# A rotary embedding on one core: storing the first batch in five parts of growing row width

## The chip, the cores and the metric

The kernel runs on one core of a Trainium2 chip. The metric is the device time of one execution in microseconds (us). "Span" is the part of it between the first and the last instruction in the trace; the device time is some 2 us longer. Ratios are computed as the mean time of one kernel's runs over that of the other's of the same rounds, so they are not quite the ratio of the medians quoted. The record gives spans to 0.1 us. The profile gives times in us from the start of the span.

## The reference

```python
x: [8, 2048, 8, 64] f32      cos, sin: [2048, 32] f32
x1, x2 = x[..., :32], x[..., 32:]
out1 = x1 * cos - x2 * sin
out2 = x1 * sin + x2 * cos
out  = concatenate([out1, out2], -1)
```

Each of the eight batches is 4 MB. The kernel must read 34.1 MB (with the tables) and write 33.6 MB.

## The kernel before

A batch lies in SBUF as 128 partitions of 8192 floats, so one row of a whole-batch DMA is 32 KB. There are five buffers, and the rotation is computed in place.

```python
HD = 512; ROW = 8192; UNIT = 2048; NBUF = 5      # floats per partition

def load(b):                                      # loads: SP queue
    for lo, n in spans([UNIT, UNIT, 2 * UNIT] if b == 0 else [ROW]):
        nc.sync.dma_start(out=xt[:, lo:lo+n], in_=xv[b, :, lo:lo+n])
        ...                                       # cos, sin after the first part

def store(b, lo, n):                              # stores: ScalarE's queue
    nc.scalar.dma_start(out=ov[b, :, lo:lo+n], in_=xts[b][:, lo:lo+n])

for b in range(NBUF): load(b)
...                                               # tables; rotate(): see below
for b in range(B):
    done = 0
    outs = list(spans([2 * UNIT, UNIT, UNIT] if b == last else [ROW]))
    for lo, n in spans(pieces(b)):                # batch 0: 2 HD, 2 HD, 3 x UNIT
        rotate(b, lo, n)
        done = lo + n
        while outs and sum(outs[0]) <= done:
            store(b, *outs.pop(0))
    if b + NBUF <= last: load(b + NBUF)           # reuses a stored buffer
```

`rotate` makes two GpSimd products with the sine (line 121), one VectorE product with the cosine (line 128) and mostly one VectorE addition back into the batch (line 135). A few pieces are added by TensorE and copied back by ScalarE.

## Time and profile before

| | before |
|---|---|
| device time, median of 6 runs | 164.25 us (164.15 to 164.58) |
| profiled span | 162.0 us |
| bytes moved | 67.65 MB |
| last VectorE instruction ends | 155.3 us |
| last store lands | 161.05 us |

The lines that carry the reading are shown in the prediction below. The page's slices cut the span in 40; a digit is the busy share in tenths. The windows table gives busy time of each engine, then the clock, the DMA share and GB/s. It books a packet at the packet's start. A packet of 32 KB takes 1.2 us, so windows of a few us scatter by some 30 GB/s around the rate. Where this document speaks of "us lost", the rate comes instead from the trace's record of each DMA packet, with its bytes spread over its duration: every stretch of 2 us between 14 and 150 us that is under 425 GB/s counts as (433 - rate)/433 x 2 us.

### The profile page before, as it was taken

To read this page: it belongs to the slowest core of one execution; us is meant where nothing else is said; L and a number is where in the kernel's file an instruction comes from. 1 tells how busy PE (TensorE), PEld (TensorE's weight loads), DVE (VectorE), ACT (ScalarE), POOL (GpSimd) and SP (SyncE) were. 2 spreads that over 40 slices of the span, in tenths; PEclk is the share of its full clock that TensorE was granted. 3 is DMA by queue.
4 is the path that set the end of the run, shared out by engine and by line. 5 is a ranking of instruction groups with operands and counts; after the bars stand their busy time and mean duration, and the time that the engine had idled before them with its cause. 6 is when DMAs were issued, how large, how long until landed. Compare 5 with 4: busy or idle time off the path is not lost.

```text
span 162.0 us, 463 instructions
## 1 busy us (share of the span) xinstructions
PE 46.6 (29%) x80; PEld 18.6 (11%) x80; DVE 140.1 (86%) x66; ACT 14.3 (9%) x24; POOL 138.9 (86%) x70
## 2 busy tenths in 40 slices
PE   0000000499008920894039913980000000000000
PEld 0000000143004400340023401330000000000000
DVE  0468999999999999999999999499989999899930
ACT  3200000013100410022001210130000000000000
POOL 1299999999999899983999979999799979999600
PEclk9999999999965997599855895799555555555555
DMA  5999999989899999999999999999999999999994
GB/s 176 419 441 494 413 388 502 372 380 429 388 477 429 396 485 413 405 494 396 421 477 396 429 463 396 453 453 388 453 447 405 445 445 405 453 437 405 417 421 198
DMA packets 3170, 67.65 MB, mean 418 GB/s; under 512 B 352, under 2 KB 352, under 8 KB 608
## 3 DMA queue, kind: packets, MB, share of 16 engines
q1 hardware_dynamic: 1728, 34.08, 49.9%
q10 hardware_dynamic: 1440, 33.56, 48.1%
q14 instruction: 2, 0.02, 0.0%
HBM read 34.08 MB, written 33.55 MB: 417 GB/s over the span
## 4 chain that ended last, share of the span: by engine, by line
DMA 47%; DVE 37%; POOL 9%; issue 2%; SPq 1%; DVEq 0%; POOLq 0%; ACTq 0%
DMA xt<-in_x_dram 26%; DVE t L128 18%; DMA out_dram<-xt 18%; DVE xt L135 17%; POOL t L121 9%; DMA sin_sb<-in_sin_dram 3%; DVE t L145 1%; SPq L69 0%; SPq L67 0%; DVEq L135 0%; POOLq L121 0%; ACTq L74 0%
## 5 line engine op out<-in xcount | busy, mean ns | idle before, releaser
L121 POOL TENSOR_TENSOR t<-xt,sin_sb 128x1024 f32<-128x1024 f32 (+1 forms) x32 | 70.5, 2203 | 12.8 <-DMA xt<-in_x_dram 6.4
L128 DVE TENSOR_TENSOR t<-xt,cos_ps 128x2048 f32<-128x2048 f32 (+1 forms) x34 | 73.4, 2167 | 0.8
L121 POOL TENSOR_TENSOR t<-xt,nsin 128x1024 f32<-128x1024 f32 (+1 forms) x32 | 70.6, 2207 | 0.0
L135 DVE TENSOR_TENSOR xt<-t,t 128x2048 f32<-128x2048 f32 (+1 forms) x29 | 62.2, 2145 | 8.1 <-POOL t L121 5.6
L140 PE MATMUL o<-t,eye 128*128 128x512 f32 x24 | 16.3, 766 | 24.0 <-DVE t L128 24.0
L156 PE MATMUL o<-t,eye 128*128 128x512 f32 x16 | 11.3, 812 | 38.1 <-DVE t L128 38.1
L141 PE MATMUL o<-t,eye 128*128 128x512 f32 x24 | 15.3, 725 | 0.0
L142 ACT COPY xt<-o 128x512 f32<-128x512 f32 x12 | 7.0, 585 | 44.8 <-PE o L141 44.8
L140 PEld LDWEIGHTS o<-t,eye 128*128 128x128 f32 x24 | 5.6, 249 | 32.5 <-issue 32.5
L156 PEld LDWEIGHTS o<-t,eye 128*128 128x128 f32 x16 | 3.8, 257 | 43.0 <-POOL t L121 30.6
L161 ACT COPY xt<-o 128x512 f32<-128x512 f32 x8 | 4.7, 586 | 44.7 <-DVE t L128 26.6
L141 PEld LDWEIGHTS o<-t,eye 128*128 128x128 f32 x24 | 5.7, 239 | 8.0 <-issue 8.0
L92 DVE COPY cos_ps<-cos_sb 128x512 f32<-128x512 f32 x1 | 0.7, 694 | 6.3 <-DMA cos_sb<-in_cos_dram 6.3
L157 PE MATMUL o<-t,neye 128*128 128x512 f32 x8 | 5.3, 766 | 0.2 <-DVE t L145 0.2
L145 DVE TENSOR_TENSOR t<-xt,sin_ps 128x2048 f32<-128x2048 f32 x2 | 4.6, 2281 | 0.0
L157 PE MATMUL o<-t,eye 128*128 128x512 f32 x8 | 4.1, 592 | 0.0
L157 PEld LDWEIGHTS o<-t,neye 128*128 128x128 f32 x8 | 1.9, 258 | 4.1 <-issue 4.1
L157 PEld LDWEIGHTS o<-t,eye 128*128 128x128 f32 x8 | 1.5, 190 | 1.9 <-issue 1.9
L89 ACT ACT_TABLE_LOAD x1 | 1.3, 1283 | 0.7 <-PEq L197 0.7
L89 ACT ACTIVATE nsin<-sin_sb 128x512 f32<-128x512 f32 x1 | 0.6, 629 | 4.9 <-DMA sin_sb<-in_sin_dram 4.9
L90 ACT COPY sin_ps<-sin_sb 128x512 f32<-128x512 f32 x1 | 0.6, 579 | 0.0
L79 POOL MEMSET eye<- 128x128 f32 x1 | 0.2, 204 | 0.3 <-POOLq L197 0.3
(6 smaller groups left out, 1.0 us busy)
## 6 DMA issues: line engine op xcount, KB each, us to landing
xt<-in_x_dram SPq DMA_DIRECT2D x7, 4096.0 KB, 42.0
out_dram<-xt ACTq DMA_DIRECT2D x7, 4096.0 KB, 25.7
xt<-in_x_dram SPq DMA_DIRECT2D x2, 1024.0 KB, 6.1
xt<-in_x_dram SPq DMA_DIRECT2D x1, 2048.0 KB, 11.5
out_dram<-xt ACTq DMA_DIRECT2D x1, 2048.0 KB, 10.8
out_dram<-xt ACTq DMA_DIRECT2D x2, 1024.0 KB, 7.1
cos_sb<-in_cos_dram SPq DMA_DIRECT2D x1, 256.0 KB, 5.1
sin_sb<-in_sin_dram SPq DMA_DIRECT2D x1, 256.0 KB, 5.3
```

The lines of the kernel that those rows point to most:

```text
L89: keep(nc.scalar.mul(nsin, sin_sb, -1.0))
L92: keep(nc.vector.tensor_copy(cos_ps, cos_sb))
L121: nc.gpsimd.tensor_mul(out=t2u[:, :, u, :].rearrange("p (r h) d -> p r h d", h=H), in0=xu[:, :, 1 - u, :].rearrange("p (r h) d -> p r h d" ...
L128: nc.vector.tensor_mul(out=t1.rearrange("p (r k d) -> p r k d", r=nr, d=Dh), in0=xk, in1=rep(cos_ps[:, r0 : r0 + nr, :], 2 * H),)
L135: keep(nc.vector.tensor_add(out=xt, in0=t1, in1=t2))
L140: nc.tensor.matmul(o, eye, t1[:, cs], start=True, stop=False)
L141: nc.tensor.matmul(o, eye, t2[:, cs], start=False, stop=True)
L142: keep(nc.scalar.copy(xt[:, cs], o))
L145: nc.vector.tensor_mul(out=t2.rearrange("p (r k d) -> p r k d", r=nr, d=Dh), in0=xk, in1=rep(sin_ps[:, r0 : r0 + nr, :], 2 * H),)
L156: nc.tensor.matmul(o, eye, t1u[:, gs, u, :], start=True, stop=False)
L157: nc.tensor.matmul(o, eye if u else neye, t2u[:, gs, 1 - u, :], start=False, stop=True)
L161: nc.scalar.copy(xu[:, gs, u, :], o.rearrange("p (g d) -> p g d", d=Dh))
```

## The change

The intent is to let the first stores begin gently beside the loads: narrow rows first, then wider ones.

```diff
             while outs and sum(outs[0]) <= done:
-                store(b, *outs.pop(0))
+                whole = outs.pop(0)
+                if b == 0:
+                    for part in spans([HD, HD, 2 * HD, UNIT, 2 * UNIT]):
+                        store(b, *part)
+                else:
+                    store(b, *whole)
```

## The prediction

> **What bounds the kernel now.** I read the page's slices first, then its queue table, then the windows table, then the waits, and last the trace's own record of each DMA packet (start, length, queue, bytes), which the views only sum up.
>
> The slices and queue table of the kernel before:
>
> ```profile
> span 162.0 us, 463 instructions
> ...
> DVE  0468999999999999999999999499989999899930
> ...
> POOL 1299999999999899983999979999799979999600
> ...
> DMA  5999999989899999999999999999999999999994
> ...
> q1 hardware_dynamic: 1728, 34.08, 49.9%
> q10 hardware_dynamic: 1440, 33.56, 48.1%
> ```
>
> The reader is to see that DMA is full in all but the first and last slice, and that the two queues (q1 carries loads, q10 stores) take 98% of the sixteen engines' span. VectorE and GpSimd are busy too, but both have holes; DMA has none.
>
> The windows table (stretch, then PE, PEld, DVE, ACT, POOL busy, clock, DMA share, GB/s):
>
> ```profile
> 8.00:28.00 20.00, 0.00 (x0) 0.00 (x0) 17.38 (x10) 0.26 (x2) 20.00 (x12) 1.00 1.02 439
> 28.00:36.00 8.00, 5.24 (x7) 2.01 (x8) 7.90 (x5) 0.58 (x1) 8.00 (x4) 1.00 0.99 377
> 36.00:132.00 96.00, 41.41 (x75) 16.59 (x73) 91.09 (x41) 11.12 (x19) 90.02 (x40) 0.75 1.01 434
> 132.00:156.00 24.00, 0.00 (x0) 0.00 (x0) 22.02 (x12) 0.00 (x0) 19.25 (x11) 0.50 0.98 424
> ```
>
> Loads alone (8 to 28), loads with stores (36 to 132) and stores alone (132 to 156) all move about the same. One stretch is low: 28 to 36 us, where the first store starts beside the loads, has 377 GB/s at a busy share of 0.99. Spread over each packet's own time, the records give 433 GB/s everywhere, but 395 in 28 to 32 and 368 in 32 to 36; that is (38 + 65)/433 x 4 = 0.95 us lost, the only real loss between start and end.
>
> The waits:
>
> ```profile
> POOL t L121 <- DMA xt<-in_x_dram: 6.4, 4, 3.4
> ...
> SPq L67 <- DMA out_dram<-xt: 76.3, 3, 38.4
> ```
>
> GpSimd waits 6.4 us for loads; the longest, 3.4 us, is for batch 4. The load queue waits 76.3 us for stores, since loads 5 to 7 reuse the buffers of batches 0 to 2. From the records, store 0 lands at 52.7, store 1 at 72.1, store 2 at 91.4, while loads 4, 5 and 6 end at 75.5, 94.9 and 114.2: each new load is queued some 23 us before the ring needs it. That wait costs nothing.
>
> The chain of waits shows store 2, load 7 (91.57 to 133.58), then batch 7's computation to 155.3. But the last three stores land at 156.2, 158.6 and 161.05, gaps of 2.4 us, the packet time of 1 MB (8 rows x 0.309 us on each engine). The transfers are back to back to the last one, so the bound is DMA, and the chain's compute runs about one microsecond ahead of it.
>
> **What the Trainium skill says.** "DMA: Bandwidth & Descriptors", Queues, rings and completion order: each engine round-robins its queue rows at packet granularity. The trace agrees, with one row of 32 KB as one packet: between 30 and 50 us the records hold 128 load and 127 store packets. The same page, Where 436 GB/s comes from, has a ceiling of 435 GB/s, near the 433 here; it also says that the HBM side, about 358, binds such transfers, which this single-core trace contradicts. The same page, Why small descriptors are slow, has a fixed overhead per packet. The trace has 84 ns for 2 KB, 309 for 8 KB, 611 for 16 KB and 1213 for 32 KB: close to 37.6 ns per KB and some 9 ns per packet. "Perfetto Trace Analysis", DMA Optimizations, says that splitting lets transfers start sooner where the engines are generally idle. Here they are not.
>
> **The change part by part.**
>
> *Bytes.* None added or removed.
>
> *Packets.* Store 0 was 8 rows of 32 KB on each engine: 8 x 1.213 = 9.70 us. Now it is 16 x 0.084 + 8 x 0.159 (4 KB, from 37.6 x 4 + 9) + 8 x 0.309 + 8 x 0.611 = 1.34 + 1.27 + 2.47 + 4.89 = 9.97 us. With four more semaphore packets of 9 ns the cost is +0.31 us, and it lies on the bound.
>
> *When the stores start.* The diff alone suggests five issues at 28.3 us. The compiled order of waits shows otherwise: each part waits for the VectorE additions of its own columns, not for the batch. In the trace of before those additions end at about 10.8, 13.4, 18.8 and (the last) 28.3, so stores start some 17 us earlier. Issues cost ScalarE 0.34 us each, and it is idle then: nothing.
>
> *Sharing the engines.* The first store packet should move near 13.5 us. From there one store row goes with each load row of 32 KB. Sixteen rounds with 2 KB rows: 16 x (1.213 + 0.084) = 20.8, to 34.3. Eight with 4 KB: 8 x 1.372 = 11.0, to 45.3. Eight with 8 KB: 8 x 1.522 = 12.2, to 57.5. The loads have 32 rows left plus the end of batch 0, so load 4 ends at about 58.5, 17 us sooner than 75.5. The rest of part 5 then runs almost alone, and store 0 lands near 63.5, 11 us later than 52.7.
>
> *New waits.* The compiled order reuses eight DMA semaphores, so load 4 is now issued only when part 2 of the store has landed (about 35), before load 3 ends (about 46): hidden. Load 5 waits for all of store 0, so the load ring stands empty from 58.5 to about 66. Store 1, issued at about 46.8, fills the engines then. Going on with 2.43 us per pair of rows, load 5 ends near 85, load 6 near 104, load 7 near 124 instead of 133.6.
>
> *Compute.* Batch 1 lands about 1 us later than 23.98, just before GpSimd wants it at 25.58: no stall by my count. The 6.4 us of waits for loads should mostly vanish, since loads 2 to 7 come earlier than before. Batch 7's computation can then end some 4 to 6 us before 155.3. But the stores are queued behind one another, and the last byte is set by total DMA work: this gain goes into a longer wait of the stores in the queue.
>
> *The start-up loss.* The 0.95 us at 28 to 36 comes when 32 KB store rows begin among 32 KB load rows: load packets stretch from 1.22 to 2.2 us before the first store packet is seen. With 2 KB rows first, this can shrink, if it scales with the row, or be spent in instalments as rows grow. I take half: -0.48 us.
>
> Sum: +0.31 - 0.48 = -0.2 us on 164.34, or 164.15 us.
>
> **The rivals.**
>
> First: the change is a real gain, because compute no longer waits for loads; batch 7's chain ends 4 to 6 us earlier and so does the kernel, near 159 to 160. For it: the chain of waits passes through load 7 and the compute. Against it: the back-to-back landings and 433 GB/s. All packets need about 157 us of each engine at the fast rates, plus about 3 us before the first packet; less than about 160 span, 162 measured, isn't there.
>
> Second: only the start-up loss moves: all of it goes and the small packets cost only 0.31, so 163.7.
>
> Third: narrow rows cost more in alternation with 32 KB rows than back to back. If each of the 32 narrow and middling rows lost 0.1 us in the switch, 3.2 us, giving 167.4. For it: no row under 8 KB is ever written to HBM in this trace, nor alternates with a long one. Against it: alternation at 32 KB costs nothing, 433 GB/s both ways.
>
> Fourth: the empty load ring between 58.5 and 66 becomes a DMA gap, or its restart repeats the start-up loss: +1 us, 165.3. Against a gap: store 1 is queued from 46.8.
>
> **Range and chances.** Rivals two and four set the range: 163.2 to 165.3. Its lower half is a little wider than runs scatter (164.15 to 164.58). Faster by over 2% needs under 161.05, beyond the whole identifiable loss: 0.02. Slower by over 2% needs over 167.6, a heavy third rival: 0.03. Within 2%: 0.95.
>
> **What would show it right or wrong.** The ScalarE queue must show five issues from about 10.8 to 28.3, not five at 28.3. Loads must carry over 80% of the bytes until about 55, and load 4 must land near 58.5. Load 7 must land near 124. GpSimd's 6.4 us of waits for loads must fall to near its first one, VectorE must end before 155, and DMA must still be full to the end. The 377 GB/s at 28 to 36 must be gone, and any dip near 13 smaller. I am wrong if DMA shows an idle slice (fourth rival), if load packets beside 2 KB stores are longer than 1.22 us (third), or if the end follows compute down (first).

## The result, and the profile after

The changed kernel takes 163.62 us (median of 6 runs, 163.56 to 163.82) against 164.25. The ratio is 0.996, 95% interval 0.9947 to 0.9973: a real gain, of 0.4%. The prediction was 164.15, range 163.2 to 165.3, and "within 2%".

The page's slices and queue table of the changed kernel:

```profile
span 161.9 us, 470 instructions
...
DVE  0468999999999999999999999999999999999600
...
POOL 1299999999999899999994999999999999996000
...
DMA  5999999999998989998999999989999999999994
...
q1 hardware_dynamic: 1728, 34.08, 49.6%
q10 hardware_dynamic: 2016, 33.56, 48.3%
```

VectorE and GpSimd stop a slice sooner than before (the zeros at the right), but DMA is full to the same slice. The stores now use 576 more packets for the same bytes.

The ScalarE queue in the timelines, first of the kernel before, then of the changed one (start, stretch, queue, line, operation, number of issues):

```profile
28.30 0.38 ACTq L74 DMA_DIRECT2D out_dram<-xt  x1
```

```profile
10.66 17.84 ACTq L74 DMA_DIRECT2D out_dram<-xt  x5
```

Five stores are issued between 10.7 and 28.5 us, as the order of waits had told; the diff alone would suggest five at 28.3.

The windows table of the changed kernel, for the same stretches as in the prediction:

```profile
8.00:28.00 20.00, 0.00 (x0) 0.00 (x0) 17.36 (x10) 0.12 (x1) 20.00 (x12) 1.00 1.04 448
28.00:36.00 8.00, 5.38 (x8) 2.11 (x9) 7.90 (x5) 0.59 (x1) 8.00 (x4) 1.00 0.98 422
36.00:132.00 96.00, 41.28 (x73) 16.49 (x72) 93.32 (x42) 11.14 (x19) 92.94 (x42) 0.72 1.00 430
132.00:156.00 24.00, 0.00 (x0) 0.00 (x0) 19.67 (x11) 0.00 (x0) 16.23 (x9) 0.50 0.98 421
```

The hole of 377 GB/s at 28 to 36 us has gone. In the third row VectorE and GpSimd have 2 to 3 us more work done by 132 us. But that row moved 434 GB/s before and now 430: something was given back there. A finer table, 44 to 60 us, first of before and then of after, finds it:

```profile
44.00:60.00 16.00, 8.77 (x16) 3.60 (x16) 15.62 (x8) 2.34 (x4) 15.47 (x7) 0.79 0.99 426
```

```profile
44.00:60.00 16.00, 10.13 (x16) 4.04 (x16) 15.62 (x8) 2.34 (x4) 15.47 (x7) 0.68 0.96 397
```

By the packet records the kernel before loses 0.92 us, all between 30 and 36 us. The changed one loses 0.52 us, all between 44 and 58 us: that is where the 4 KB store rows give way to 8 KB rows beside the loads (at 46.3), and up to where load 4 ends. The 16 KB rows begin only then, at 57.6, so they hardly meet a load. There the 32 KB load packets have a median of 1.241 us, with single ones up to 1.57, against 1.213 elsewhere. Beside the 2 KB store rows (253 load packets and 256 store packets in 14.5 to 34.3 us) they stay at 1.213.

The waits of the changed kernel, where those of before had a line of 6.4 us for GpSimd on loads of x:

```profile
POOL t L121 <- DMA sin_sb<-in_sin_dram: 5.6, 1, 5.6
POOL t L121 <- DVE xt L135: 2.6, 2, 2.2
```

The line of 6.4 us has disappeared; of GpSimd's waits for DMA only the start is left, the wait for the sine table. But GpSimd now waits 2.6 us for VectorE, where it waited 0.5 before. It ends 4.1 us sooner (148.2 against 152.3), and VectorE, on which the stores wait, 2.8 us sooner (152.5 against 155.3).

The chain of waits, its first line for each kernel, before and then after:

```profile
DMA 47%; DVE 37%; POOL 9%; issue 2%; SPq 1%; DVEq 0%; POOLq 0%; ACTq 0%
```

```profile
DVE 75%; POOL 9%; issue 6%; DMA 3%; SPq 0%; DVEq 0%; POOLq 0%
```

A reader could conclude that VectorE now bounds the kernel. The chain follows the last store back to the instruction that released its issue. It does not show that the store then waited behind other stores. VectorE ends at 152.5 us, and the last three stores land at 156.1, 158.5 and 161.0, still 2.4 us apart. The pair of delay runs below tests this.

Landings from the semaphore records, against the prediction:

| lands at, us | before | predicted | after |
|---|---|---|---|
| load 4 | 75.5 | 58.5 | 58.4 |
| store 0, all parts | 52.7 | 63.5 | 63.2 |
| load 5 | 94.9 | 85 | 86.2 |
| load 6 | 114.2 | 104 | 106.3 |
| load 7 | 133.6 | 124 | 125.8 |
| last store | 161.05 | | 160.97 |

The schedule turned upside down (load 7 comes 8 us sooner) and the last byte moved by 0.08 us in the profiled runs.

**Two parts of the gain.** Each run gives its device time and its span. The six runs of the changed kernel have a mean span of 161.85 us and 1.80 us outside it (1.76 to 1.83). Eleven runs of the kernel before in the first series below have 162.08 and 2.15 (2.08 to 2.20). So, as far as spans rounded to 0.1 us tell, some 0.23 us of the gain lies in the span and some 0.35 us outside it, in time that the profile does not show. The experiments address both.

### The profile page after: what moved, and what is told of

Same layout as the page of the kernel before. It is cut to its first block, busy times and chain, and to the rows that moved or that the text cites. A ratio compares the mean times of both kernels' runs of the same rounds, so it can differ in the third digit from the quotient of the medians.

```text
span 161.9 us, 470 instructions
## 1 busy us (share of the span) xinstructions
PE 46.7 (29%) x80; PEld 18.6 (11%) x80; DVE 140.1 (87%) x66; ACT 14.4 (9%) x24; POOL 139.0 (86%) x70
## 4 chain that ended last, share of the span: by engine, by line
DVE 75%; POOL 9%; issue 6%; DMA 3%; SPq 0%; DVEq 0%; POOLq 0%
DVE t L128 40%; DVE xt L135 33%; POOL t L121 9%; DMA sin_sb<-in_sin_dram 3%; DVE t L145 3%; DVEq L135 0%; SPq L69 0%; SPq L67 0%; POOLq L121 0%
```

## The experiments

Theory A: the span's gain comes from the loss at the turn from loads to stores (0.92 us before, 0.52 after), less 0.31 us for narrow packets. Theory B: it comes from stores that begin sooner or from compute that waits less. All eleven kernels gave correct results. Times are means, with those of the kernel before in the same rounds. Executions over 1.5% slower than the fastest of the same kernel are left out of the means.

### Growing widths, but late

```diff
-                    for part in spans([HD, HD, 2 * HD, UNIT, 2 * UNIT]):
+                    store(b, 15 * HD, HD)          # waits for the whole batch
+                    for part in spans([HD, 2 * HD, UNIT, 2 * UNIT]):
                         store(b, *part)
```

> The five widths of the change (2, 2, 4, 8, 16 KB rows), but all of them held until batch 0 is computed, by sending the last 2 KB of each row first. Theory A (the gain is the start-up loss: load rows stretch when long store rows begin among them, and narrow rows make that loss small): the loss at 28 to 36 us (0.95 us before) is gone here too, because load 4 ends at about 54 us, before the 8 and 16 KB rows begin. Narrow packets cost 0.3 us, so about 0.6 us under the kernel before, 163.6 us, and every 2 us window from 14 to 150 us at 425 GB/s or more. Theory B (the gain is that stores begin 17 us earlier, or that compute waits less): no earlier start here, so 164.2 to 164.5 us.

Measured: 164.13 us against 164.23, ratio 0.9994 (0.9979 to 1.001). One run of six was at 164.76; the median is 164.01. Theory A's 163.6 was missed. The windows table of this run:

```profile
28.00:36.00 8.00, 5.23 (x8) 2.02 (x9) 7.90 (x5) 0.59 (x1) 8.00 (x4) 1.00 1.09 468
48.00:56.00 8.00, 6.93 (x10) 2.95 (x11) 7.76 (x5) 0.86 (x2) 7.56 (x5) 0.56 0.96 367
```

The hole at 28 to 36 is gone, as theory A said, but 0.80 us is lost at 50 to 56, as load 4 ends and only stores are left. Theory A in its simple form (long rows that begin beside loads) is wrong: the store rows here are 2 and 4 KB when the loss comes. Theory B's 164.2 to 164.5 is nearer; the mean and the median lie under it by 0.1 and 0.2 us.

### Two parts of 16 KB rows

```diff
-                    for part in spans([HD, HD, 2 * HD, UNIT, 2 * UNIT]):
+                    for part in spans([2 * UNIT, 2 * UNIT]):
```

> Batch 0 stored in two parts of 16 KB rows, the first about 9 us earlier than before (18.8 us). Theory A: store rows start at 16 KB beside loads, and 32 KB rows of store 1 follow at about 51 us, still beside load 4. If the loss goes with the step in row size, it is spent in two instalments and sums to about the same 0.9 us: no gain, 164.2 us. If it goes with the first row only, half of it: 163.8 us. Theory B (earlier start is the gain): between before and the change, some 163.9 us. The two dips, at about 21 and 51 us, tell the first from the others.

Measured: 163.61 us (four runs, median 163.54; a fifth at 168.8 was slow) against 164.23, ratio 0.9962 (0.9949 to 0.9976), as good as the change. There is one dip, 0.70 us at 20 to 24, and none at 51. Neither form of theory A had the sum right, and theory B's 163.9 was missed too: the loss is smaller than with 32 KB rows, and widening the rows to 32 KB later, with load 4 still running, cost nothing. Its windows table:

```profile
20.00:24.00 4.00, 0.00 (x0) 0.00 (x0) 3.86 (x3) 0.00 (x0) 4.00 (x3) 1.00 0.86 295
28.00:36.00 8.00, 5.22 (x8) 2.07 (x9) 7.90 (x5) 0.59 (x1) 8.00 (x4) 1.00 1.02 438
48.00:56.00 8.00, 6.92 (x10) 3.05 (x11) 7.76 (x5) 1.10 (x2) 8.00 (x5) 0.59 1.06 459
```

### Four parts of 8 KB rows

```diff
-                    for part in spans([HD, HD, 2 * HD, UNIT, 2 * UNIT]):
+                    for part in spans([UNIT] * 4):
```

> Batch 0 stored in four parts of 8 KB rows, from 13.4 us. Packets cost 32 x 0.309 - 9.70 = 0.19 us. Theory A: one start with 8 KB rows, a dip of 0.1 to 0.2 us near 16 us, and since 32 store rows meet about 31 load rows, the 32 KB rows of store 1 begin only when load 4 has ended, with no second dip. Then 0.95 - 0.15 - 0.19 = 0.6 us under before, 163.6 us, no worse than the change. If what counts is to begin with the narrowest row, it is worse than the change: 163.9 us.

Measured: 164.40 us (163.62 to 165.03) against 164.23, ratio 1.001 (0.9985 to 1.0034), above both expected figures. The dips are small, 0.49 us in all, spread over 16 to 38 us and 78 to 80. Yet the spans scatter from 161.8 to 163.1. The trace has the reason for its own run: the first and the last of the sixteen engines to finish the last store are 1.85 us apart, against 1.04 us in the kernel before. A store is done when its slowest engine is. The first three parts of store 0 already land with 1.9 to 2.1 us between engines; the gap falls to 0.83 at its last part, which ends just after load 4, and is 2.55 at store 1, when loads run again. Why some engines fall behind here is open.

### No store while loads run

Row size stays at 32 KB. Fixed buffers; store 0 goes behind load 4 on the load queue, store 1 is issued after the first half of batch 2.

```diff
-    keep(nc.scalar.dma_start(out=ov[b, ...], in_=xts[b][...]))
+    q = nc.sync if b == 0 else nc.scalar
+    keep(q.dma_start(out=ov[b, ...], in_=xts[b][...]))
 ...
+            if b == 2 and lo == UNIT:
+                store(1, 0, ROW)
+                load(1 + NBUF)
```

> Row size left at 32 KB. Store 0 is put behind load 4 on the load queue and store 1 is issued only after the ScalarE work of batch 2, so that no store starts while a load is moving; fixed buffers. Store 0 then begins at about 52 us, 20 us later than before. Theory A: no start-up loss and no narrow packets: 0.95 us under before, 163.3 us, with 433 GB/s in all windows from 14 to 150 us, the fastest of all. Theory B (stores must start early, or narrow rows help in themselves): 164.2 us or slower.

Measured: 163.75 us against 164.23, ratio 0.9971 (0.9959 to 0.9983), span 161.96. That is faster than before, but by 0.12 us in the span and not by 0.95. The windows table shows where the expected gain went:

```profile
28.00:36.00 8.00, 5.28 (x8) 2.08 (x9) 7.90 (x5) 0.59 (x1) 8.00 (x4) 1.00 1.04 446
48.00:56.00 8.00, 6.98 (x10) 3.03 (x11) 7.76 (x5) 1.15 (x2) 7.60 (x5) 0.60 1.00 393
```

Nothing is lost at 28 to 36; 0.68 us is lost at 50 to 54, where loads end and the first store follows on the same queue, and 0.28 at 76 to 80. The second dip comes as store 1 ends (75.9 to 77.7 us), some 8 us after the loads have set in again (68 us). Load and store rows need not alternate for the loss to come.

### The delay test, before and after

```diff
+        if b == last:
+            for _ in range(4):
+                keep(nc.gpsimd.tensor_mul(out=cos_sb, in0=sin_sb, in1=sin_sb))
         for lo, n in spans(pieces(b)):
```

In the kernel before:

> The kernel before with 5.0 us of idle GpSimd work (4 products of 128x512 into a table that is no longer read, 1.26 us each) put ahead of batch 7. In the kernel before, GpSimd waits about 1.1 us for load 7 at that point and the last store is issued about 1 us before DMA could take it. Theory DMA-bound with thin compute slack: about 5.0 - 1.1 = 3.9 us later compute, 2.8 to 3.5 us of it seen in the time: 167.0 to 167.8 us.

In the changed kernel:

> The same 5.0 us ahead of batch 7 in the changed kernel. VectorE there ends at about 151 us, some 4 us sooner than before, and the last store waits in the queue. Theory DMA-bound (the compute gain was turned into slack): the delay is taken up by the slack, compute ends at about 156 us, and the time rises by at most 1 us: 163.6 to 164.6 us. Rival (the end follows compute): the full 5 us, 168.6 us.

Measured: before with the delay 165.89 us against 164.27, ratio 1.0098 (1.0075 to 1.0122). The changed kernel with the delay takes 163.83 against 164.27, ratio 0.9973 (0.9956 to 0.9991); without it the ratio was 0.996. The four products took 4.40 us, not 5.0, as the GpSimd timeline of the second run shows:

```profile
129.75 4.40 POOL L178 TENSOR_TENSOR cos_sb<-sin_sb 128x512 f32<-128x512 f32 x4
```

The last VectorE addition of the kernel before, then with the delay:

```profile
154.05 1.23 DVE L135 TENSOR_TENSOR xt<-t,t 128x1024 f32<-128x1024 f32 x1
```

```profile
157.49 1.23 DVE L135 TENSOR_TENSOR xt<-t,t 128x1024 f32<-128x1024 f32 x1
```

And of the changed kernel, then with the delay:

```profile
151.23 1.23 DVE L135 TENSOR_TENSOR xt<-t,t 128x1024 f32<-128x1024 f32 x1
```

```profile
154.44 1.23 DVE L135 TENSOR_TENSOR xt<-t,t 128x1024 f32<-128x1024 f32 x1
```

Compute ends 3.4 us later in the one pair and 3.2 us later in the other. The first pays 1.6 us for it, the second about 0.2. The end of the changed kernel does not follow VectorE, whatever its chain of waits says, and the compute gain has become slack. My figure for the first kernel was too high because its slack is larger than the 1 us I had read: with the queue empty, the last 1 MB store lands 3.9 us after VectorE's end, where it took 5.8 before.

### A narrow head alone

```diff
-                    for part in spans([HD, HD, 2 * HD, UNIT, 2 * UNIT]):
+                    for part in spans([HD, ROW - HD]):
```

> Batch 0 stored in two parts: 2 KB rows as soon as the first addition is done, then 30 KB rows when the batch is done. Theory of instalments (the loss comes with the turn of the traffic from loads to stores, whatever came before): nothing is lost at the 2 KB rows, and 0.8 to 0.95 us near 30 to 34 us as before; span 162.0 to 162.2. Theory of the first row (only the first store row beside loads costs): no dip near 30, span about 161.2. Early start as such: span 161.85 as the changed kernel.

Measured: 163.94 us against 164.25, ratio 0.9978 (0.9964 to 0.9993), but the span is 162.12 against 162.11. The windows table:

```profile
28.00:36.00 8.00, 5.16 (x8) 2.04 (x9) 7.90 (x5) 0.59 (x1) 8.00 (x4) 1.00 0.99 362
48.00:56.00 8.00, 6.86 (x10) 3.02 (x11) 7.79 (x4) 1.06 (x2) 7.54 (x5) 0.59 1.01 438
```

The 2 KB rows cost nothing, and 1.23 us is lost when the 30 KB rows come. Neither "only the first row counts" nor "an early start counts" holds. The loss comes as the traffic turns to stores, and it begins before the first long store packet is recorded: by the packet records the rate is 331 GB/s at 30 to 32 us, where no store packet is recorded yet, and 306 at 32 to 34, where stores have a third of the bytes. In the version with two parts it is 306 GB/s at 22 to 24, with 3% of the bytes in stores. All the gain of this kernel lies outside its span (1.81 us).

### Controls for the time outside the span

Idle ScalarE work, DMA unchanged: one or four times

```diff
     keep(nc.scalar.mul(neye, eye, -1.0))
+    for _ in range(4):                # or range(1)
+        keep(nc.scalar.mul(neye, eye, -1.0))
```

The kernel before with four and with one more instruction:

> Control: the kernel before with four more ScalarE instructions of 0.3 us in a stretch in which ScalarE is idle, and no DMA changed. In the runs so far the time outside the profiled span is 2.08 to 2.20 us for the kernel before and 1.76 to 1.83 us for the changed one, 0.35 us that no DMA theory explains. If this part goes with the length of the ScalarE program, it falls to about 1.8 here with the span still at 162.1, so 163.9 us. If it comes from the DMA arrangement, it stays at 2.1 and the time at 164.25 us.

> Control: the same with one more ScalarE instruction instead of four, as the version with two parts has. Length of the program: 1.8 outside the span, as that version had (1.76 to 1.85). DMA arrangement: 2.1, 164.25 us.

The changed kernel with one and with four:

> Control: the changed kernel with one more ScalarE instruction of 0.3 us in an idle stretch of ScalarE; DMA unchanged. Span 161.85 as the changed kernel. If the 1.76 to 1.83 us outside the span belong to its DMA arrangement they stay; if they go with how the program happens to lie, they move, to anything between 1.75 and 2.2.

> Control: the changed kernel with four more such instructions. Span 161.85. DMA arrangement: 1.76 to 1.83 outside the span, 163.6 us in all. Program layout: may differ, up to 164.0.

Measured (device time; span; outside, as means with the range of the last):

| kernel | time | span | outside |
|---|---|---|---|
| before, 7 runs | 164.27 | 162.11 | 2.15 (2.12 to 2.21) |
| before + 4 | 164.22 | 162.25 | 1.97 (1.77 to 2.10) |
| before + 1 | 164.00 | 162.03 | 1.97 (1.95 to 1.99) |
| changed, 6 runs | 163.65 | 161.85 | 1.80 (1.76 to 1.83) |
| changed + 1 | 163.77 | 161.95 | 1.82 (1.78 to 1.84) |
| changed + 4 | 163.84 | 162.03 | 1.82 (1.76 to 1.86) |

The last two rows were run beside seven other runs of the kernel before, with 164.25, 162.11 and 2.14.

An instruction that no DMA sees moves the outside time of the kernel before by 0.18 us, about half of the 0.35. (The four GpSimd products of the delay test left it at 2.16.) So this time is not a pure result of how the DMAs are arranged. But the changed kernel keeps 1.8 with padding, and every kernel that splits or moves store 0 has 1.8 to 1.95. What this time is stays open; nothing in the traces shows it.

### All versions together

Packet cost is the time of store 0's packets beyond the 9.70 us of before. It is worked out as in the prediction, 9 ns for each added semaphore packet included, with 0.159 us now measured for the 4 KB row and 1.138 us for the 30 KB row. Turn loss is from the records of the profiled run, and so is the last column: when the last store landed, as the mean over the sixteen engines and for the last of them.

| store 0 | turn loss | packet cost | sum | span, mean (median) | last store, mean engine (last engine) |
|---|---|---|---|---|---|
| before | 0.92 | 0 | 0.92 | 162.08 (162.1) | 160.35 (161.05) |
| five growing (the change) | 0.52 | 0.31 | 0.83 | 161.85 (161.8) | 160.04 (160.97) |
| two of 16 KB | 0.70 | 0.08 | 0.78 | 161.80 (161.7) | 160.13 (160.85) |
| held behind load 4 | 0.96 | 0 | 0.96 | 161.96 (162.0) | 160.43 (161.00) |
| growing, late | 0.80 | 0.31 | 1.11 | 162.18 (162.05) | 160.36 (161.02) |
| 2 KB, then 30 KB | 1.23 | 0.08 | 1.31 | 162.12 (162.1) | 160.60 (161.25) |
| four of 8 KB | 0.49 | 0.21 | 0.70 | 162.47 (162.35) | 160.21 (161.53) |

The sums differ by 0.6 us at most. The spans follow them only roughly, but the mean engine follows them well: the three smallest sums have the three earliest means, and the largest sum has the latest. The last engine then adds between 0.57 us (held) and 1.32 us (four of 8 KB), which is as much as the versions differ by, and that is why "four of 8 KB" is out of order by span.

One profiled run carries each row, but the padded and delayed kernels repeat the first two: their added work is on other engines and, where it delays anything, comes after 128 us. Four traces with the transfers of before lose 0.92, 1.16, 1.02 and 1.04 us at 30 to 36; four with those of the change 0.52, 0.65, 0.51 and 0.59 in all. The mean engine lands at 160.35 to 160.47 (three traces; the delayed one has its end moved) against 160.04 to 160.26 (four). So the smaller loss repeats, and the means, 0.28 us apart, agree with a span gain of some 0.2 us. Theory A holds in this sense: as a sum of loss and packet cost. Theory B is not supported: the held version starts its stores latest and is not slower, the narrow head starts early and keeps the span of before, and the delay test shows that compute had slack. No version clearly beats the change; two parts of 16 KB equal it with less code.

## Why the prediction was right

*The bound.* Right. DMA stayed full, and the compute gain turned into waiting in the store queue, and the delay test shows that slack directly. The size of the compute gain was too high: VectorE ended 2.8 us sooner (152.5), not 4 to 6, as GpSimd exchanged a part of its waits for loads for waits for VectorE. The first rival (a gain of 4 to 5 us through compute) fell with that.

*When the stores start.* Right, from the compiled order: issues from 10.7 us. The first store packet came at 14.6, where I had 13.5.

*Sharing.* Right to within 2.3 us in all five landings (load 6 is the furthest off), by counting one store row for one load row. The loads' share was 94% of the bytes up to 48 us (91% from 14 us on, when stores run too), and 79% in 48 to 56, where I had asked for over 80%.

*Packets.* Right. Every 2 KB store packet took 84 ns in alternation with 32 KB load packets, every 4 KB one 159. The third rival, a cost of switching, is not there at these sizes.

*New waits.* Right: the load ring stood empty between load 4 and load 5 and stores filled the engines at 432 to 433 GB/s. The fourth rival's gap did not come, nor a loss at the restart of the loads in the changed kernel.

*Start-up loss.* Half was a guess between "shrinks" and "in instalments". It measured 0.40 us of gain (0.92 to 0.52), or 0.47 as the mean of four traces each, where I had 0.48; that a guess came so close is luck. The runs do not choose between its two reasons. For a loss that scales with the row speak the starts with 8, 16 and 32 KB rows (0.49, 0.70 and 0.92 to 1.16 us); against it the late version, which loses 0.80 us beside rows of 2 and 4 KB. A narrow head alone saves nothing. What makes the turn cost is not shown.

*The sum.* For the span I had 0.31 - 0.48 = -0.17 us. The packet terms give 0.31 - 0.40 = -0.09 (-0.16 with the mean of four traces), and the mean spans -0.23 (-0.15 over all 14 runs with the changed DMAs, padded ones included: mean 161.93). The step that was missing is another: I took the device time as the span and a constant. Some 0.35 us of the 0.6 lie outside the span, in a part that no step of the prediction named. So the time is right for its range, and the larger part of the small gain is unexplained. That the range held is in part luck. I wrote that rivals two and four set it, but rival two gives 163.7, and no sum shown there leads down to the lower end of 163.2. The measured 163.62 lies under rival two, and inside the range only because of that spare half microsecond. My -0.2 us was also set on 164.34, the median of the first three runs; on the 164.25 of all six it gives 164.05.

## What to carry to other kernels

Here every DMA engine was full and the transfers landed back to back, and a better order of transfers moved waits by many microseconds and the end by a few tenths. In such a case count packets and bytes before hoping for the compute that no longer waits. Narrow rows beside wide ones are a real lever on the share that each queue gets, because the engines alternate row by row here, and the schedule that follows could be worked out by hand to 2.3 us. A chain of waits that names an engine is a claim to test with a delay, and gains of a few tenths should be split into span and outside before they are given a cause.

## What the Trainium skill lacked or had wrong

- "DMA: Bandwidth & Descriptors", Where 436 GB/s comes from: says that the HBM side, about 358 GB/s, binds transfers between HBM and SBUF. With one core active these runs moved 433 GB/s in load, store and mixed stretches, so here the port ceiling of 435 is the one to plan with. The skill is not wrong as a whole: the Roofline section of "Perfetto Trace Analysis" makes this exception for a core that streams alone; the sentence misleads only where it is read without it.
- "DMA: Bandwidth & Descriptors", Queues, rings and completion order: gives a packet as some 9 to 17 descriptors. In these records the queues alternate by single rows of each width tried, from 2 to 32 KB (253 load rows of 32 KB beside 256 store rows of 2 KB). How many descriptors such a row has, the records do not show.
- In the pages read I found no cost for the turn from loads to stores: 0.5 to 1.2 us per kernel in these profiled runs, paid once or in instalments.
- "Perfetto Trace Analysis", DMA Optimizations: its advice to split is for idle engines, and for DMA-bound kernels its first point advises larger transfers. It lacks the case of this kernel: with full engines, a split into five, two of them with rows of 2 KB, moved a load's landing by up to 17 us, and the kernel was 0.4% faster, not slower.
- "Runtime: NRT & Kernel Launch", The ~15µs preamble/postamble breakdown, lists work around the kernel whose total depends on engine count and DMA setup, but nothing in it explains a time outside the traced span of 1.76 to 2.21 us that moves with the kernel, and no run here ties that time to one of its stages.
